# A two-layer encoder trunk on one core: weight splits issued at points from a table, seven products combined in banks by ScalarE copies, first products behind products of the identity

## The chip, the core and the metric

The kernel runs on one of the eight cores of a Trainium2 chip. A core has TensorE (PE, matrix products), VectorE (DVE), ScalarE (ACT), GpSimd (POOL) and SyncE (SP), each with its own queue of instructions, worked off in order. TensorE writes into PSUM, eight banks of 128 partitions x 512 f32; everything else lies in SBUF. Loads and stores are DMAs, issued here mostly by SP, a few by ACT, and those that add to what they find ("accumulating") by POOL.

The metric is the device time of one execution in microseconds, less is better. Before the change it is 919.12 us, the median of three runs (917.77 to 919.91).

## What is computed

256 tokens of width 1024 pass two layers in f32. A layer is half an FFN step, an attention step with two kinds of heads, and another half FFN step; a last normalization follows.

```python
for l in range(DEPTH):                                   # 2
    x = x + 0.5 * swiglu(rms_norm(x, g1), w_gate, w_up, w_down)      # D_FF = 2816
    h = rms_norm(x, mix_norm[l]); proj = h @ w_in[l]                 # q, k, v of both kinds of heads
    x = x + concat([windowed_gqa_sink(...), differential_attention(...)]) @ w_out[l]
    x = x + 0.5 * swiglu(rms_norm(x, g2), w_gate, w_up, w_down)
return rms_norm(x, final_norm)
def swiglu(h, w_gate, w_up, w_down):
    return (silu(h @ w_gate) * (h @ w_up)) @ w_down
```

So there are four FFNs, and they hold most of the products.

## The kernel before

**Split products.** To keep f32 accuracy at the faster format, every operand is split into a high part (ACT casts it, `emit_split`, line 211) and a low part (DVE subtracts the cast from the original, line 212), and a product is made of three matmuls: high x high, low x high, high x low (`tokens`, lines 537 to 539; `prod`, lines 632 to 634). Each weight is loaded once, in blocks of 1 MB (4 chunks of 128 rows x 512 columns); a block is one `Step`, split in two halves ("parts"), each one ACT instruction and one DVE instruction over 128 x 1024.

**Order of the weights.** `specs` is the list of all steps in the order of use. `weights()` (line 249) hands out the next one and calls `ahead(n)` (line 228), which issues, in order of the list, the splits up to part n, the preparations and the DMAs (at most 10 steps ahead and 6 raw blocks at once). How far splits run ahead is one number, `look[0]`: 8 in an FFN, 6 in the attention, with corrections at single places (`less`). `Split.part` (line 182) calls `ahead` once more at the second half of a block.

**Seven products.** FF = 2816 columns are worked in five groups of 512 and a rest of 256. In the groups that `SEVEN` names (2, 3, 4 in the first FFN, 1 to 4 in the other three; 15 in all) the four quarter products of (two blocks of 128 tokens) x (two halves of the inner dimension) for gate and up together are made with seven products of combinations in place of eight. The combinations of x are made once an FFN (`make_sums`, line 349); those of the weights are the blocks a, a+b, b+c, a+b+c and so on, made by accumulating DMAs on POOL (`gather`, line 126) and by DVE adds over 128 x 1024, two a block (`plus`, line 131). `by_seven` (line 637) makes the products in banks of their own, copies two of them to SBUF with ACT (`m1`, `m7`) and combines them with five DVE instructions (`put`, lines 679 to 686) and two that multiply with the silu (`up`, line 616). A group is seven products of 12 matmuls, two down-products of 24 matmuls of the group before (`down`, line 708), and eight transposes of the hidden values (`turn`, line 694), which ACT and DVE split again.

**Banks.** `bank()` (line 71) gives one of eight banks. The four of the down-product (`accs`, line 706) are held through an FFN.

**The start.** ACT's queue issues the four DMAs of x (line 425), 256 KB each, while SP loads the first two weight blocks in chunks of 256 KB (`emit_dma`, lines 155 to 157). `take_x` (line 441) then turns x: for chunks 0 and 1, four transposes each on TensorE, then the operands by ACT (scaled by the gain, line 333) and DVE (line 335); the first products (line 722) come after both. The first Silu comes much later, and with it its table.

**Scheduling.** TensorE's order is always the program's (`Kept`, line 40); that of the other engines too, but for the attention (`kept[0] = False`, line 901), where a scheduler orders them.

Of the kernel before, what the change touches and what calls it, by code (L numbers as in the profile page):

```python
# [9 lines left out]
F32 = mybir.dt.float32  # L10
F32R = mybir.dt.float32r
AF = mybir.ActivationFunctionType
# [18 lines left out]
SEVEN = ((2, 3, 4), (1, 2, 3, 4))  # L31


@with_exitstack
def trunk(ctx: ExitStack, tc: tile.TileContext, x, n1, g1, u1, d1, nm, w_in, sink,
# [35 lines left out]
    def bank():  # L71
        return ps.tile([P, 512], F32, tag="ps", bufs=8, name=nm_("ps"))
# [19 lines left out]
    class Step:  # L92
        def __init__(self, kn, n, moves, key=None, prep=None, src=None, free=None, behind=None):
            self.kn, self.n, self.moves, self.prep = kn, n, moves, prep
            self.behind = behind
            self.key = object() if key is None else key
            self.src = self.key if src is None else src
            self.free = [self.src] if free is None else free
# [16 lines left out]
    def seven(wg, wu, c0, downs, first):  # L115
# [22 lines left out]
        bc = Step(4, 512, load(b), key=b, behind=gather(c, b))  # L138
        rest = [Step(4, 512, load(d), key=d, free=[]), Step(4, 512, load(c), key=c, free=[]), downs[0]]
        steps = [rest[0], rest[2], rest[1], bc] if first else [bc] + rest  # L140
# [3 lines left out]
                Step(4, 512, None, prep=plus(c, a), src=a, free=[c]),  # L144
                Step(4, 512, None, prep=plus(d, a), src=a, free=[a, d]),
                downs[1]]
# [29 lines left out]
    class Split:  # L176


        def __init__(self, i):
            self.i, self.n, self.parts, self.held = i, specs[i].n, [], False  # L180

        def part(self, k, c=slice(None), h=None):

            if h is None:
                h, k = divmod(k, 2)
            if h and not self.held:
                self.held = True
                ahead(2 * self.i + 1 + look[0])
            return [t[:, k, c] for t in self.parts[h]]
# [38 lines left out]
    def ahead(n):  # L228

        n = min(n, 2 * len(specs) - 1)  # L230
        while True:
            if at["split"] <= n and at["prep"] > at["split"] // 2:
# [3 lines left out]
            elif at["prep"] <= min(n // 2 + 1, len(specs) - 1) and at["dma"] > at["prep"] and \  # L236
                    (specs[at["prep"]].prep is None or at["split"] >= 2 * at["prep"]):
# [10 lines left out]

    def weights(less=0, held=False):

        i = at["use"]
        at["use"] += 1
        if i > 1:
            ahead(2 * i + look[0] - less)
        w = loaded[i]
        w.held = held
        return w

    for l in range(DEPTH):
        def ffn_specs(wg, wu, wd, sevens):  # L260
            down = lambda g, h: plain(wd[l], h * 512, 512, 4 * g, 4)
            for k0 in (0, 4):
                specs.extend(plain(w[l], 0, 512, k0, 4) for w in (wg, wu))
            for g in range(1, NGRP):
                downs = [down(g - 1, h) for h in range(2)]
                if g in sevens:
                    specs.extend(seven(wg[l], wu[l], g * 512, downs, g == 1))
                else:
                    specs.extend(plain(w[l], g * 512, 512, k0, 4) for w in (wg, wu) for k0 in (0, 4))
                    specs.extend(downs)  # L270
# [6 lines left out]
            specs.append(down(NGRP - 1, 1))  # L277

# [21 lines left out]
        fine.update(range(mixed + 2, len(specs)))  # L300
        ffn_specs(g2, u2, d2, SEVEN[1])

# [3 lines left out]
    class Norm:  # L306
# [21 lines left out]
        def operands(self, j, sl):  # L328
# [3 lines left out]
            for i, g in enumerate(gs):  # L332
                act.activation(xs[:, i, 0:S], sl[:, i], AF.Identity, scale=g)
            for i, g in enumerate(gs):
                dve.scalar_tensor_tensor(xs[:, i, S:512], in0=sl[:, i], scalar=g, in1=f(xs[:, i, 0:S]),
                                         op0=ALU.mult, op1=ALU.subtract)
            self.turned.append((j, sl, gs))
# [11 lines left out]
        def make_sums(self):  # L349
# [19 lines left out]
            s1 = add(b1, t1, ALU.subtract)  # L369
            s2 = add(s1, t0, ALU.add)  # L370
            yield
            high(s1)
            high(s2)
            yield
            low(0, s1)
            b0_ = add(b0, s2, ALU.subtract)
            low(1, s2)
            v = add(t1, t0, ALU.subtract)
            yield
            high(b0_)  # L380
            high(v)
            yield
            low(2, b0_)
            low(3, v)
# [38 lines left out]
    early = [emit_early(0), emit_early(1)]  # L423
    for j in range(4):
        act.dma_start(xk[:, :, j * 256:(j + 1) * 256], x[0].rearrange("(t p) d -> p t d", p=P)[:, :, j * 256:(j + 1) * 256])
        for e in early:
            next(e)

# [12 lines left out]
    def take_x(k):  # L441

        g, u = early
        if k == 0:
            for j in (0, 1):
                sl = norm.turn(j)
                next(g)
                norm.operands(j, sl)
                next(u)
        elif k == 1:  # L450
            for e in (g, u, g, u):
                next(e)
            norm.squares(0, 0, 512)
            norm.pair(2)
            norm.squares(1, 0, 512)
            ahead(5)
            norm.pair(3)
            norm.squares(0, 512, 512)
        elif k == 2:
            for e in early:  # L460
                next(e, None)
            ahead(7)
            norm.squares(1, 512, 512)
            norm.stats()
            constants()
# [63 lines left out]

    def tokens(accs, xs, w, k0, ks=range(4), first=0, last=KC - 1, order=None, cols=slice(None), h=None):  # L530

        for k, t in (order or [(k, t) for k in ks for t in range(2)]):
            kk = k0 + k
            hi, lo = w.part(k, cols, h)
            xv = xs[kk // 2][:, kk % 2]
            xh, xl = xv[:, t * P:(t + 1) * P], xv[:, S + t * P:S + (t + 1) * P]
# [23 lines left out]
    def first_groups(norm, ws):  # L560

        sls = [halves(bank()) for _ in ws]
# [39 lines left out]
    def ffn(norm, aside=None, before=None, final=False, sevens=SEVEN[1]):  # L602
# [34 lines left out]
        def by_seven(h, g):  # L637


            flat = lambda: tmp().rearrange("p a n -> p (a n)")  # L640

            def put(o, x, y, op):
                dve.tensor_tensor(o, x, y, op=op)
                return o

            late, run = g == max(sevens), 1 in sevens
            m1, m7 = flat(), flat()


            if g > 1:  # L650
                g0 = prod(norm.quarter(0, 0), weights())
                act.copy(m1, g0)
                p7 = prod(norm.summed(3), weights(1, True))
                act.copy(m7, p7)
                hT = turn(h, 2)
                prod(norm.quarter(0, 1), weights(), g0)
                p3 = prod(norm.summed(2), weights())
                if not run:
                    g0 = silu(flat(), g0, 0)
                down(hT, g - 1, 0, weights())  # L660
                if run:
                    g0 = silu(flat(), g0, 0)
            else:
                p1 = prod(norm.quarter(0, 0), weights(1, True))
                hT = turn(h, (0,))
                w = weights(1, True)
                act.copy(m1, p1)
                p2 = prod(norm.quarter(0, 1), w)
                hT += turn(h, (1,))
                g0 = put(flat(), p2, m1, ALU.add)  # L670
                down(hT, 0, 0, weights())
                silu(g0, g0, 0)
                p3 = prod(norm.summed(2), weights())
                p7 = prod(norm.summed(3), weights(1, True))
                act.copy(m7, p7)
# [486 lines left out]
```

## Time and profile before

| | |
|---|---|
| median of three runs | 919.12 us (917.77 to 919.91) |
| the profiled execution | 917.39 us |
| its span, first to last instruction | 915.6 us |
| mean granted TensorE clock | 0.999 |
| HBM read | 199.00 MB, 218 GB/s over the span |

A line of the groups' view reads: line, engine, operation, output tile <- input tiles, shapes, count | busy us, mean ns of one | idle us of the engine just before, and what ended it. In the timeline a line has start, duration and engine, and equal instructions that follow each other are one line with a count. In the chain of waits a line has start, length and what was waited for or ran. In the windows' view each engine has its busy time and, in brackets, its instructions that touch the window. PE is the matmul, PEld the load of its stationary operand, "w" a split weight, "s" a split operand or a hidden value, "raw" a loaded block, "tmp" a combination, "ps" a bank. Nearly every instruction has line 50, that of the helper which records them, so one goes by tiles.

### The profile page before, as it was taken

What the parts mean: (1) busy time and instruction counts of PE and PEld (TensorE: products, weight loads), DVE (VectorE), ACT (ScalarE), POOL (GpSimd) and SP (SyncE); (2) the same over time, 40 slices, a digit from 0 to 9 for tenths busy, and PEclk for the clock granted to TensorE, in tenths of its full rate; (3) what the DMA queues carried; (4) which work ended last, traced back from release to release, by engine and by line L of the source; (5) the groups of instructions that cost most, each with busy time, mean ns of one, the idle gap of its engine ahead of it and who ended that gap; (6) DMA issues with size and microseconds to landing.
All of it is one profiled execution on the core that took longest, in us unless ns stands there. A gap on an engine that the chain in (4) does not pass through costs nothing.

```text
span 915.6 us, 12544 instructions
## 1 busy us (share of the span) xinstructions
PE 904.5 (99%) x4696; PEld 763.7 (83%) x4696; DVE 792.5 (87%) x1096; ACT 589.8 (64%) x917; POOL 66.4 (7%) x83
## 2 busy tenths in 40 slices
PE   8999999999999999999999999999999999999997
PEld 6888888899888888888888888888998888888886
DVE  6768999959975999999789999997797689999994
ACT  7836676557865766576486666665677496666561
POOL 0400100000010100100010010000001010010011
PEclk9999999999999999999999999999999999999999
DMA  9996898828436698898767998887463467998831
GB/s 339 355 238 173 265 297 268 238 93 240 136 108 189 158 280 248 257 273 275 258 164 201 276 285 217 265 293 219 116 230 98 139 153 201 275 289 230 259 132 47
DMA packets 114061, 200.87 MB, mean 219 GB/s; under 512 B 3662, under 2 KB 31376, under 8 KB 114000
## 3 DMA queue, kind: packets, MB, share of 16 engines
q1 hardware_dynamic: 96528, 166.74, 54.5%
q0 software_dynamic: 16096, 31.75, 19.3%
q10 hardware_dynamic: 1376, 1.57, 0.5%
q8 instruction: 37, 0.61, 0.3%
q14 instruction: 24, 0.20, 0.1%
HBM read 199.00 MB, written 1.05 MB: 218 GB/s over the span
## 4 chain that ended last, share of the span: by engine, by line
PE 98%; issue 1%; DMA 0%; ACT 0%; DVE 0%; POOLq 0%; POOL 0%; ACTq 0%
PE ps L50 98%; DMA xk<-in_x_dram 0%; ACT w L50 0%; DVE s L50 0%; DVE xk L50 0%; ACT tmp L50 0%; ACT L50 0%; POOLq L1157 0%; POOL rf L50 0%; ACTq L50 0%; DVE tot L50 0%; DVE tmp L50 0%
## 5 line engine op out<-in xcount | busy, mean ns | idle before, releaser
L50 PE MATMUL ps<-w,s 128*128 128x512 f32 (+1 forms) x2574 | 600.2, 391 | 0.5 <-ACT tmp L50 0.5
L50 PEld LDWEIGHTS ps<-w,s 128*128 128x128 f32 x2574 | 477.6, 188 | 100.3 <-ACT tmp L50 2.3
L50 DVE TENSOR_TENSOR w<-raw,w 128x1024 fp32r<-128x1024 f32 (+1 forms) x458 | 482.1, 1101 | 37.8 <-ACT w L50 36.6
L50 ACT CAST w<-raw 128x1024 fp32r<-128x1024 f32 (+1 forms) x458 | 409.8, 954 | 122.6 <-DVE raw L50 78.4
L50 PE MATMUL ps<-w,q 128*128 128x512 f32 x540 | 127.3, 389 | 0.0
L50 PEld LDWEIGHTS ps<-w,q 128*128 128x128 f32 x540 | 101.4, 188 | 21.0
L50 PE MATMUL ps<-s,w 128*128 128x256 f32 x672 | 83.1, 284 | 0.0
L50 PEld LDWEIGHTS ps<-s,w 128*128 128x128 f32 x672 | 81.5, 192 | 0.5
L50 POOL DMA_DIRECT2D raw<-in_ffn_w_up_dram x30 | 38.9, 1296 | 472.8 <-DVE w L50 240.8
L50 DVE TENSOR_TENSOR raw<-raw,raw 128x1024 f32<-128x1024 f32 x60 | 70.7, 1219 | 0.0
L50 ACT ACTIVATE s<-ps,gcol 128x256 fp32r<-128x256 f32 (+1 forms) x80 | 31.7, 480 | 43.7 <-PE ps L50 42.1
L50 ACT CAST s<-ps 128x512 fp32r<-128x512 f32 x44 | 24.3, 594 | 29.9 <-PE ps L50 29.9
L50 PE MATMUL ps<-w,v 128*128 128x512 f32 x180 | 43.3, 389 | 0.0
L50 ACT COPY tmp<-ps 128x512 f32<-128x512 f32 x34 | 19.9, 585 | 36.2 <-PE ps L50 34.0
L50 ACT ACTIVATE s<-s,negm 128x256 f32<-128x256 f32 x64 | 31.9, 500 | 14.8 <-DVE negm L50 14.8
L50 PE MATMUL ps<-ident,s 128*128 128x128 f32 x304 | 39.7, 273 | 0.0
L50 PEld LDWEIGHTS ps<-w,v 128*128 128x128 f32 x180 | 33.8, 188 | 7.0
L50 PEld LDWEIGHTS ps<-ident,s 128*128 128x128 f32 x304 | 35.1, 140 | 5.1 <-issue 0.8
L50 DVE TENSOR_TENSOR s<-ps,s 128x512 fp32r<-128x512 f32 x44 | 28.7, 686 | 9.1 <-ACT s L50 9.1
L50 DVE SCALAR_TENSOR_TENSOR s<-ps,gcol,s 128x256 fp32r<-128x256 f32 x48 | 20.3, 478 | 11.6 <-ACT s L50 11.5
L50 DVE TENSOR_TENSOR tmp<-ps,tmp 128x512 f32<-128x512 f32 x37 | 25.4, 686 | 2.7 <-PE ps L50 2.1
L50 DVE TENSOR_TENSOR xk<-xk,ps 128x512 f32<-128x512 f32 (+1 forms) x25 | 14.1, 598 | 14.9 <-PE ps L50 14.9
(106 smaller groups left out, 404.7 us busy)
## 6 DMA issues: line engine op xcount, KB each, us to landing
raw<-in_ffn_w_down_dram SPq DMA_DIRECT2D x44, 1024.0 KB, 8.9
raw<-in_ffn_w_gate_dram SPq DMA_DIRECT2D x39, 1024.0 KB, 6.4
raw<-in_ffn_w_up_dram SPq DMA_DIRECT2D x39, 1024.0 KB, 5.7
raw<-in_ffn_w_up_dram POOLq DMA_DIRECT2D x30, 1024.0 KB, 12.3
raw<-in_w_in_dram SPq DMA_DIRECT2D x14, 1024.0 KB, 6.1
raw<-in_ffn_w_gate_dram SPq DMA_DIRECT2D x8, 512.0 KB, 6.2
raw<-in_ffn_w_up_dram SPq DMA_DIRECT2D x8, 512.0 KB, 7.2
raw<-in_w_in_dram SPq DMA_DIRECT2D x8, 512.0 KB, 5.3
```

The source lines that it names most:

```text
L50: ins = issue(*a, **k)
```

## The change

1. **Table of leads.** `LEAD` replaces the one number at named places: a step has `lead = (name, n)`, and `lead()` calls `ahead(2 * i + LEAD[name][2 * n + half])`; inside the seven products `go()` calls it eleven times a group with the next value. `ahead` also holds a split back while an accumulating DMA is still pending.
2. **Seven products in banks.** Six banks stay single (`bank()`), two become one pair (`pair()`). The first product p1 is copied by one ScalarE instruction, negated and broadcast, into both banks of the pair; two later products add there. p1 takes its second product in its own bank, then is overwritten by a ScalarE copy of p5 from bank to bank, and the last product adds to that. DVE makes three combinations in place of five. `plus` is one add over 128 x 2048, block c is loaded later, the transposes go by token (`turn_one`), and the down-product of the second half moves into the next group (`below`), so that it stands between the transposes of the first and the second token block. The signs of the combined x (`make_sums`) change with it. In the FFNs whose first such group is group 1, that group has no earlier one to take a down-product from, and its order is p1, eight transposes, the second product into p1. The pair is also used for other two-bank places in FFN and attention.
3. **The start.** x's first chunk stays on ACT's queue, the other three go to SP, behind four, eight and eight of the weight chunks. A one-element Silu on ACT loads the table. Four products identity x identity go ahead of the transpose of the gains, one after it, two after the transposes of x's chunk 0; then the products of chunk 0 follow (`first_chunk`, in the order high, weight's low, x's low), and only then chunk 1 is turned. The later chunks are turned between products too.

```diff
+LEAD = dict(start=(2, 8, 11, 9),
...
+            mid=(6, 9, 9, 12, 15, 15, 17, 20, 20, 23, 24),
...
     def bank():
-        return ps.tile([P, 512], F32, tag="ps", bufs=8, name=nm_("ps"))
+        return ps.tile([P, 512], F32, tag="ps", bufs=6, name=nm_("ps"))
+
+    def pair():
+        return ps.tile([P, 2, 512], F32, tag="xy", bufs=1, name=nm_("xy"))
...
             def prep():
-                for h in (0, 2):
-                    x_, t_ = [raws[i][:, h:h + 2] for i in (x, to)]
-                    dve.tensor_tensor(t_, t_, x_, op=ALU.add)
+                dve.tensor_tensor(raws[to], raws[to], raws[x], op=ALU.add)
...
+    fetch_x(act, 0)
+    tables = const.tile([P, 1], F32, name="tables")
+    act.activation(tables, ident[:, 0:1], AF.Silu)
     for j in range(4):
-        act.dma_start(xk[:, :, j * 256:(j + 1) * 256], x[0].rearrange("(t p) d -> p t d", p=P)[:, :, j * 256:(j + 1) * 256])
         for e in early:
             next(e)
+        if j == 1:
+            fetch_x(sp, 1)
+    for j in (2, 3):
+        fetch_x(sp, j)
...
+    def keep_busy(n):
+        for _ in range(n):
+            pe.matmul(warm[:, 0:P], lhsT=ident, rhs=ident, start=True, stop=True)
...
+    keep_busy(4)
     pe.transpose(gsl[:, 0:16], grow1, ident[:16, :16])
+    keep_busy(1)
...
+                go()
+                p1 = prod(norm.quarter(0, 0), take())
+                act.activation(xy, p1.unsqueeze(1).to_broadcast([P, 2, 512]), AF.Copy, scale=-1.0)
+                new = [turn_one(h, 0)]
+                go()
+                if start:
+                    new.append(turn_one(h, 1))
+                    go()
+                    prod(norm.quarter(0, 1), take(), p1)
+                else:
+                    below(old, g - 2, 1, take())
+                    new.append(turn_one(h, 1))
+                    go()
+                prod(norm.summed(0), take(), xy[:, 0])
+                go()
+                below(by_token(new), g - 1, 0, take())
+                go()
+                if not start:
+                    prod(norm.quarter(0, 1), take(), p1)
+                g0 = silu(flat(), p1, 0)
+                go()
+                old = by_token(new)
+                p5 = prod(norm.summed(1), take())
+                act.copy(p1, p5)
+                go()
+                prod(norm.summed(2), take(), xy[:, 1])
+                go()
+                prod(norm.summed(3), take(), p5)
+                e = flat()
+                act.copy(e, p5)
+                u1, u0 = flat(), flat()
+                dve.tensor_tensor(u0, xy[:, 1], e, op=ALU.add)
+                dve.tensor_tensor(u1, xy[:, 0], e, op=ALU.add)
+                h = blk(F32)
+                up(h, u0, g0, 0)
+                go()
+                p4 = prod(norm.quarter(1, 1), take(), p1)
+                g1 = flat()
+                dve.tensor_tensor(g1, p4, u1, op=ALU.subtract)
+                go()
+                silu(g1, g1, 1)
+                up(h, u1, g1, 1)
+                go()
```

More of the change, by code (lines that the diff above doesn't have):

```diff
@@ L113, in plain, with seven @@
         return Step(kn, n, lambda t: [(t, src)], **how)
-    def seven(wg, wu, c0, downs, first):
+    def seven(wg, wu, c0, below, down):
         a, b, c, d = [object() for _ in range(4)]
@@ L247, in ahead, with lead @@
                 break
+    def lead(i, half, less=0):
+        s = specs[i]
+        if s.lead is not None:
+            ahead(2 * i + LEAD[s.lead[0]][2 * s.lead[1] + half])
+        else:
+            ahead(2 * i + half + look[0] - less)
     def weights(less=0, held=False):
@@ L253, in weights @@
         if i > 1:
-            ahead(2 * i + look[0] - less)
+            lead(i, 0, less)
+            ahead(2 * i + 1)
         w = loaded[i]
@@ L560, in first_groups @@
     def first_groups(norm, ws):
-        sls = [halves(bank()) for _ in ws]
+        both = pair()
+        sls = [halves(both[:, i]) for i in range(2)]
         for k in range(0, KC, 2):
@@ L937, in mix @@
         vB = tp.tile([P, 2, 512], F32, tag="v", bufs=1, name=nm_("v"))
-        vsl = [bank() for _ in range(2)]
+        both = pair()
+        vsl = [both[:, t] for t in range(2)]
         for k0 in (0, 4):
@@ L984, in mix @@
         oT = [blk() for _ in range(4)]
-        rsl, osl = [[bank() for _ in range(2)] for _ in range(2)]
+        rsl, both = [bank() for _ in range(2)], pair()
+        osl = [both[:, t] for t in range(2)]
         for t in range(2):
```

262 lines of the change are left out of this document (157 added, 105 removed).

## The prediction

> **What bounds the kernel now.** I read the page's first section first (who is busy), then the chain of waits (what the end is made of), then the timeline of the start, because only there does the chain leave TensorE.
>
> ```profile
> span 915.6 us, 12544 instructions
> ...
> PE 904.5 (99%) x4696; PEld 763.7 (83%) x4696; DVE 792.5 (87%) x1096; ACT 589.8 (64%) x917; POOL 66.4 (7%) x83
> ```
>
> ```profile
> 5.70 22.17 PE ps L50 x96
> ...
> 29.00 0.65 ACT L50
> ...
> 30.30 0.70 ACT tmp L50
> ...
> 31.04 873.94 PE ps L50 x4547
> ```
>
> TensorE is busy 99% of the span, and from 31.04 us the chain is one piece of TensorE, 873.94 us long. So an engine made faster elsewhere buys nothing by itself; only fewer TensorE instructions, a faster pace, or shorter pauses count. The instruction orders of the two programs hold the same 3258 products of 512 columns, 902 of 256 columns and the same transposes; the changed one has seven identity products more. TensorE's work does not shrink, so I look for pauses.
>
> ```profile
> 1.01 0.29 POOL masks.py:199 TENSOR_SCALAR_AFFINE_SELECT ident<-ident 128x128 f32<-128x128 f32 x1
> ...
> 3.13 0.26 PE L50 MATMUL ps<-ident,grow 16*128 16x16 f32 x1 [3.13 <-DMA grow<-in_ffn_norm_dram]
> ...
> 3.74 1.12 PE L50 MATMUL ps<-ident,xk 128*128 128x128 f32 x4 [0.35 <-DMA xk<-in_x_dram]
> ...
> 4.99 0.62 ACT L50 CAST w<-raw 128x512 fp32r<-128x512 f32 x1 [0.91 <-DMA raw<-in_ffn_w_gate_dram]
> 5.51 0.83 ACT L50 ACTIVATE s<-ps,gcol 128x256 fp32r<-128x256 f32 x2
> ...
> 5.70 1.11 PE L50 MATMUL ps<-ident,xk 128*128 128x128 f32 x4 [0.85 <-DMA xk<-in_x_dram]
> ...
> 6.47 5.74 PE L50 MATMUL ps<-w,s 128*128 128x512 f32 x19
> ```
>
> ```profile
> 13.18 1.03 PE L50 MATMUL ps<-ident,xk 128*128 128x128 f32 x8
> ...
> 13.97 16.61 PE L50 MATMUL ps<-w,s 128*128 128x512 f32 x72
> ...
> 29.00 1.28 ACT L50 ACT_TABLE_LOAD   x1
> ...
> 31.04 5.30 PE L50 MATMUL ps<-w,s 128*128 128x512 f32 x22 [0.46 <-ACT tmp L50]
> ```
>
> ```profile
> core 0: us, PE busy (x) PEld busy (x) DVE busy (x) ACT busy (x) POOL busy (x), PEclk, DMA share, GB/s
> 6.47:9.08 2.61, 2.61 (x8) 2.01 (x7) 1.88 (x4) 1.63 (x4) 0.00 (x0) 1.00 1.06 399
> 9.08:11.69 2.61, 2.61 (x13) 2.16 (x12) 2.56 (x6) 2.50 (x5) 0.00 (x0) 1.00 1.06 389
> 344.70:375.50 30.80, 30.80 (x141) 25.61 (x140) 30.48 (x32) 19.96 (x24) 2.57 (x2) 1.00 0.92 266
> ```
>
> The first product starts at 6.47 us. Eight matmuls fall in the 2.61 us up to 9.08 and thirteen in the next 2.61 us, so TensorE starts at about half pace, although the clock column says 1.00 in both. The third row is one seven-product group in the steady state: TensorE has no pause, VectorE is busy 30.48 of 30.80 us and still does not hold it up.
>
> **The change part by part.** The pace of one product comes from these rows, and with it the price of the new waits:
>
> ```profile
> 340.87 2.88 PE L50 MATMUL ps<-w,v 128*128 128x512 f32 x12
> ...
> 343.59 1.03 PE L50 MATMUL ps<-ident,s 128*128 128x128 f32 x8
> 343.79 0.59 ACT L50 COPY tmp<-ps 128x512 f32<-128x512 f32 x1 [2.13 <-PE ps L50]
> ...
> 344.38 0.94 PE L50 MATMUL ps<-w,s 128*128 128x512 f32 x3
> ```
>
> Twelve products take 343.59 - 340.87 = 2.72 us, 0.227 each; eight transposes 344.38 - 343.59 = 0.79 us; ScalarE reads a finished bank 0.20 us after the last slot ends.
>
> *The start.* The common point is "24 first products and eight transposes of x done". Before, that is 13.18 us: 6.47 plus 24 x 0.227 = 5.45, plus 1.26 lost to the half pace. After, the order is: five identity products around the transpose of the gains, four transposes of x, two identity products, then the products of chunk 0, and only then the other four transposes. Identity is ready at 1.30. An identity product in f32 is not in the trace; the nearest is
>
> ```profile
> L50 PE MATMUL ps<-v,s 128*128 128x128 f32 x64 | 7.5, 275 | 0.0
> ```
>
> whose 64 records stand for 32 instructions, so two passes each, 7.5/32 = 0.23 us at full pace and perhaps 0.45 at half: four end by 3.15, which is when the gains' DMA lands anyway (3.13); one more, the gains and four transposes at half pace (1.12) end by 5.0, two more by 5.8. All seven cost about 3 us of TensorE, beside the wait for the DMA and for ScalarE, which sets the first product. That one needs the first weight chunk (landed 4.99, a cast of 0.62) and one ScalarE operand (0.83/2 = 0.42). Chunks of 256 KB land 0.7 us apart (4.99, then x's second at 5.70), and x's second to fourth chunk leave ScalarE's queue for SP's, behind four and eight weight chunks; so the first weight chunk comes between 4.3 and 4.99. I take 4.5, so 5.54, and 5.7 with the identity products in front (bounds 5.4 and 6.1). From there 5.45 + 0.44 (four transposes at full pace, 0.11 each) + what half pace is left. TensorE found full pace at about 9.1, 3.4 us after steady work began at 5.70; with work from 1.35 that comes between 4.8 and 8.2, at most (8.2 - 5.7)/2 = 1.25 lost, and I take 0.4. So 12.0 against 13.18: **1.2 us gained** (bounds 0 and 1.9). x's last chunks on SP are not late: all twelve chunks are 3.1 MB, some 8 us at the 389 GB/s of the row above, so there by 12; the transposes that need them stand at 14 and later.
>
> The Trainium skill, "TensorE: Matmul & The Clock Gate", section "What's actually happening", has the array at half clock until one window of about 3.4 us was busy, and the window runs free of the kernel's start. This trace agrees with the 3.4 us; by that rule the identity products save 0 to 1.26 us from run to run, and the sum would be 0.4 better or 0.85 worse, which lies inside the bounds above.
>
> *The Silu table.* Before, 72 products from 13.97 would end at 13.97 + 16.34 = 30.31; TensorE goes on at 31.04, after the table load at 29.00 and the two silus, whose bank it wants. After, a dummy Silu loads the table while ScalarE waits for the first DMA, one load fewer in all, and the silus stand ahead of the casts that waited for a later weight. **0.7 us gained** (0 to 0.73).
>
> *Seven products.* Before, VectorE makes five combinations a group, after, three; ScalarE's copies rise from two of 512 to one of 1024 and two of 512.
>
> ```profile
> 369.57 0.69 DVE L50 TENSOR_TENSOR tmp<-tmp,ps 128x512 f32<-128x512 f32 x1
> 370.29 1.42 DVE L50 SCALAR_TENSOR_TENSOR s<-tmp,hr,tmp 128x512 f32<-128x512 f32 x2
> 371.62 4.63 DVE L50 TENSOR_TENSOR w<-raw,w 128x1024 fp32r<-128x1024 f32 x4
> 376.16 0.69 DVE L50 TENSOR_TENSOR s<-ps,s 128x512 fp32r<-128x512 f32 x1
> ```
>
> By starts, a split costs (376.16 - 371.62)/4 = 1.135, a combination 0.7, a final multiply 0.67. A group has 9 weight blocks: 18 splits 20.4, four half sums (or two whole ones) 4.5, two multiplies 1.35, two subtractions 1.3, and 5 x 0.7 = 3.5 before, 31.1 in all against TensorE's 30.8; after, 3 x 0.7 = 2.1, 29.7. Thirty combinations, 21 us of VectorE, go, and nearly nothing of it is on the path. What is:
>
> ```profile
> PEld ps L50 <- ACT tmp L50: 2.3, 5, 0.9
> ...
> PEld ps L50 <- DVE w L50: 1.2, 4, 0.4
> ```
>
> The four waits for a split, 1.2 us in all, are where VectorE's debt comes due. I take **0.6 us gained** (0 to 1.2), as a weight load's wait is in part hidden by the matmul before it.
>
> *The new wait.* In the first group of the second, third and fourth FFN the copy of -p1 into both banks of the pair must end before the second product adds to p1, and only eight transposes lie between. The copy starts 0.20 after p1, lasts as long as the nearest row of that size,
>
> ```profile
> L50 ACT CAST w<-raw 128x1024 fp32r<-128x1024 f32 x354 | 352.3, 1053 | 120.5 <-DVE raw L50 78.4 <-DMA raw<-in_ffn_w_up_dram 40.3
> ```
>
> 1.05, and 0.05 later TensorE may go (30.30 + 0.70 to 31.04): 1.30 - 0.79 = 0.5 us, three times: **1.5 us lost** (0 if the copy takes half, 4 if ScalarE comes a cast late each time). Behind it on TensorE stands everything; behind the copy on ScalarE the copies of the transposes, needed 5 us later. In all other groups 24 products lie between, 5.4 us, and the wait is covered.
>
> *The whole sums.* One sum of 2048 in place of two of 1024: the cast can't start after the first half, so VectorE idles one cast, 1.0 us, after the second sum of a group: 29.7 + 1.0 = 30.7 against 30.8. It still fits; cost taken as 0, bounds under the rival below. The pair of banks takes two of the eight, used where before two plain banks were; the order of TensorE in the attention is unchanged; the leads from tables shift splits by a few places and I take 0 (-0.3 to +1).
>
> **Sum:** -1.2 - 0.7 - 0.6 + 1.5 = -1.0 us. The profiled execution took 917.39 us (its span of 915.6 and 1.8 around it), so 916.4; that execution is 1.73 under the median of the three runs, 919.12, on which the forecast is put: **918.1 us**.
>
> **The rivals.** *The new wait is covered and the clock is early* (the copy between banks quicker than a cast, first weight chunk at 4.3): -1.5 - 0.4 - 0.3 on the forecast, and up to 0.6 more from the splits: 915.3 to 915.9. Against it: no row has a copy into a bank of that size. *VectorE's order becomes the bound:* slower. Two groups on, the next group's first transposes want the bank of p1, freed when VectorE has made the last combination; by my count that is ready 3.6 us after the sixth product's end and wanted 5.4 us after it, but five splits stand ahead of it in VectorE's order, behind the whole sum; that leaves about 1.1 us. It decides once a group runs over 30.8 us on VectorE: at 0.7 over, the second handover of a run pays 0.3, the third 0.7; at 1.0 over, 0.9 and 1.0. With three runs of four and one of three that is 3.3 to 6.6 us: 921.4 to 924.7. For it: 30.7 of 30.8. Against it: before stood at 31.1 and paid 1.2. *An added DMA holds the cast ahead of the copies:*
>
> ```profile
> raw<-in_ffn_w_up_dram POOLq DMA_DIRECT2D x30, 1024.0 KB, 12.3
> ```
>
> it takes 12.3 us, and ScalarE already waited 40.3 us for those blocks without TensorE's minding; now silu and the copies stand behind, room about 2 us; 0.3 us in eleven groups gives 921.4. *Nothing of it shows:* the start gains 0 as the chunks land as before, the rest cancels: 919.
>
> **How the numbers follow.** Forecast 0.50 (own range 917.0 to 919.2), covered wait 0.22, VectorE's order 0.18, DMA 0.05, nothing 0.05. About 0.2% (1.84 us) is what a measurement of this kernel can tell from no change, so faster means under 917.3. Of the forecast's half, 0.16 lies under that and the rest within; so faster 0.38, same 0.39 and slower 0.23. The range goes from 915.6 to 922.5 and leaves out the dearer half of VectorE's case and little below.
>
> **What would show it.** Right: the first product near 5.7 at full pace soon after, no table load near 29, VectorE about 20 us less busy, and after the first group's eight transposes a TensorE wait of 0.5 us for ScalarE, three times. Wrong: waits for VectorE at the transposes that follow a group, growing along a run; casts waiting for an added DMA with TensorE idle behind; splits late in the attention.

## The result: 916.61 us, and the profile after

| | before | after |
|---|---|---|
| median of 20 runs side by side | 917.89 us (916.69 to 921.05) | 916.61 us (916.06 to 918.08) |
| profiled execution | 917.39 us | 916.47 us |
| its span | 915.6 us | 914.7 us |

The ratio is 0.9982 (95% interval 0.9975 to 0.9988): the change saves 1.65 us of 917.89, 1.1 to 2.3 by the interval; the two medians alone lie 1.28 us apart. The forecast was 1.0 us saved, 918.1 us. Most of the 1.5 us between 918.1 and 916.61 lies in the base: the three runs shown had a median of 919.12, the twenty 917.89. For the profiled execution the forecast was 916.4, and 916.47 came.

The page's first section after the change (the helper line is now 62):

```profile
span 914.7 us, 12449 instructions
...
PE 906.1 (99%) x4710; PEld 766.4 (84%) x4710; DVE 767.5 (84%) x1033; ACT 600.1 (66%) x932; POOL 66.9 (7%) x83
```

TensorE has fourteen records more (seven identity products of two passes) and is as full as before; VectorE has lost 25 us, ScalarE gained 10. As forecast, neither tells where the time came from. The timeline of the start does:

```profile
4.44 0.62 ACT L62 CAST w<-raw 128x512 fp32r<-128x512 f32 x1 [1.71 <-DMA raw<-in_ffn_w_gate_dram]
...
5.79 2.09 PE L62 MATMUL ps<-w,s 128*128 128x512 f32 x6
...
12.31 1.52 PE L62 MATMUL ps<-w,s 128*128 128x512 f32 x6
...
27.28 1.27 ACT L62 ACTIVATE tmp<-ps,r 128x512 f32<-128x512 f32 x2 [0.47 <-POOL r L62]
...
29.56 1.75 PE L62 MATMUL ps<-w,s 128*128 128x512 f32 x7
```

The first product starts at 5.79 (before 6.47). Twenty-four products and eight transposes are done at 12.31 (before 13.18): 0.87 us gained. The silus come at 27.28 without a table load, and the products that stood at 31.04 stand at 29.56: 1.48 us in all, so 0.61 more between the two points.

The windows of the start and of one steady group, with the instructions of each engine in brackets:

```profile
core 0: us, PE busy (x) PEld busy (x) DVE busy (x) ACT busy (x) POOL busy (x), PEclk, DMA share, GB/s
5.79:8.40 2.61, 2.61 (x11) 2.14 (x10) 2.36 (x5) 2.06 (x4) 0.00 (x0) 1.00 1.00 346
8.40:11.01 2.61, 2.61 (x15) 2.16 (x14) 0.92 (x2) 1.27 (x4) 0.00 (x0) 1.00 1.01 352
344.70:375.50 30.80, 30.80 (x141) 25.51 (x140) 29.58 (x28) 21.96 (x26) 2.57 (x2) 1.00 0.91 261
```

From the first product on, eleven matmuls fit in 2.61 us, where before eight did; the half pace ends sooner, and again the clock column does not show it. The trace's own record of the granted clock says why: it begins only where the pace first doubles, at 6.75 us here and at 8.89 before, and the column counts what lies ahead of the record as 1.00. In the steady group VectorE is busy 29.58 of 30.80 us (before 30.48), and TensorE has no pause.

What was paid back stands in the view of waits and, for the first of three places, in the timeline:

```profile
PEld ps L62 <- ACT xy L62: 1.4, 3, 0.5
...
ACT w L62 <- DMA raw<-in_ffn_w_up_dram: 11.2, 2, 10.9
```

```profile
308.28 1.03 PE L62 MATMUL ps<-ident,s 128*128 128x128 f32 x8
308.48 1.01 ACT L62 ACTIVATE xy<-ps 128x1024 f32<-128x1024 f32 x1 [3.35 <-PE ps L62]
309.40 1.08 ACT L62 CAST s<-ps 128x512 fp32r<-128x512 f32 x2
...
309.54 2.79 PE L62 MATMUL ps<-w,s 128*128 128x512 f32 x11 [0.23 <-ACT xy L62]
```

The copy of -p1 lasts 1.01 us; the product behind the eight transposes starts at 309.54, 1.26 after the first of them in place of 0.79: 0.47 us, three times, 1.4 in all. The four waits of weight loads for a split (1.2 us) are gone from the view, and so is most of ScalarE's waiting for the blocks of w_up (40.3 to 11.2 us).

### The profile page after: what moved, and what is told of

Same layout as the page of the kernel before. It is cut to its first block, busy times and chain, and to the rows that moved or that the text cites. A ratio compares the mean times of both kernels' runs of the same rounds, so it can differ in the third digit from the quotient of the medians.

```text
span 914.7 us, 12449 instructions
## 1 busy us (share of the span) xinstructions
PE 906.1 (99%) x4710; PEld 766.4 (84%) x4710; DVE 767.5 (84%) x1033; ACT 600.1 (66%) x932; POOL 66.9 (7%) x83
## 3 DMA queue, kind: packets, MB, share of 16 engines
HBM read 199.00 MB, written 1.05 MB: 219 GB/s over the span
## 4 chain that ended last, share of the span: by engine, by line
PE 98%; issue 0%; ACT 0%; DVE 0%; POOL 0%; POOLq 0%
PE ps L62 73%; PE xy L62 26%; ACT xy L62 0%; DVE s L62 0%; DVE xk L62 0%; POOLq L1291 0%; POOL rf L62 0%; POOL ident masks.py:199 0%; POOL ident masks.py:197 0%; DVE tot L62 0%; POOLq masks.py:199 0%; DVE tmp L62 0%; POOLq L1282 0%
## 5 line engine op out<-in xcount | busy, mean ns | idle before, releaser
L62 PE MATMUL ps<-w,s 128*128 128x512 f32 (+1 forms) x2046 | 478.1, 390 | 0.7 <-ACT xy L62 0.7
L62 PEld LDWEIGHTS ps<-w,s 128*128 128x128 f32 x2046 | 379.4, 188 | 78.9 <-ACT xy L62 1.4
L62 PE MATMUL xy<-w,s 128*128 128x512 f32 x528 | 125.8, 392 | 0.0
L62 PEld LDWEIGHTS xy<-w,s 128*128 128x128 f32 x528 | 98.3, 188 | 20.4
L62 PE MATMUL xy<-w,q 128*128 128x512 f32 x360 | 87.8, 393 | 0.0
L62 PEld LDWEIGHTS xy<-w,q 128*128 128x128 f32 x360 | 66.7, 188 | 13.4
L62 DVE TENSOR_TENSOR raw<-raw,raw 128x2048 f32<-128x2048 f32 x30 | 68.6, 2288 | 0.5
L62 PE MATMUL ps<-s,w 128*128 128x256 f32 x480 | 59.2, 284 | 0.0
L62 PE MATMUL ps<-w,q 128*128 128x512 f32 x180 | 43.2, 389 | 0.0
L62 PEld LDWEIGHTS ps<-w,q 128*128 128x128 f32 x180 | 33.8, 188 | 7.0
```

Source lines behind the costliest of these rows:

```text
L62: ins = issue(*a, **k)
```

## The experiments

All start from the changed kernel. Where a time is set against "the changed kernel", that is 916.61 us (20 runs) or 916.53 (12 more runs, below). The twelve runs were made in three sets of four, each on a chip of its own (first the two engines, the copy twice, no identity products and no early table; last two more instructions, half sums, flat leads and the old order), and the changed kernel was repeated in the second set alone. The kernel before had medians of 918.62, 918.66 and 918.21 us beside them, 917.89 in the result above, so a few tenths of a microsecond between sets prove nothing. The profiles say more: set product by product, behind the start, TensorE's starts in two profiles of these versions keep one distance, within 0.02 us over hundreds of products, and it steps where a wait differs.

**Two engines for the copy.**

```diff
-  act.activation(xy, p1.unsqueeze(1).to_broadcast([P, 2, 512]), AF.Copy, scale=-1.0)
+  if start:
+      act.activation(xy[:, 0], p1, AF.Copy, scale=-1.0)
+      dve.tensor_scalar_mul(xy[:, 1], p1, -1.0)
```

> Theory (the changed kernel pays the new wait in full, 0.5 us at each of three places; with ScalarE copying -p1 into one bank of the pair and VectorE into the other side by side, 0.6 to 0.7 us each in place of 1.01, the copies end with the eight transposes): the three TensorE waits for the copy fall from 0.46 to under 0.1 us, the time falls by 1.0 to 1.5 us on the changed kernel's 916.6, to 915.1 to 915.6. Rival (two engines that read one bank at once slow each other, or VectorE comes late to its copy, so the wait only changes its name): a wait of 0.4 to 0.7 us for VectorE at the same three places, 916.4 to 917.2.

Measured: 917.45 us (916.96 to 917.97), 0.8 more than the changed kernel. The timeline of the first place:

```profile
307.83 1.03 PE L62 MATMUL ps<-ident,s 128*128 128x128 f32 x8
308.03 0.58 ACT L62 ACTIVATE xy<-ps 128x512 f32<-128x512 f32 x1 [3.35 <-PE ps L62]
...
308.64 0.70 DVE L62 TENSOR_SCALAR xy<-ps 128x512 f32<-128x512 f32 x1 [0.66 <-ACT xy L62]
...
309.40 1.89 PE L62 MATMUL ps<-w,s 128*128 128x512 f32 x7 [0.53 <-DVE xy L62]
```

The copies do not run side by side: VectorE waits 0.66 us for ScalarE's and starts when that is over, so 0.58 + 0.70 stand in place of 1.01, and TensorE starts 1.57 after the first transpose in place of 1.26. Three times 0.31 is 0.9: product by product TensorE falls back by 0.31 at each of the three places and nowhere else behind the start, and 0.8 is the time measured. The Trainium skill, "PSUM — Partial Sum Buffer", section "PSUM bank collisions raise a hardware error", says that two engines must not use the same 32-partition quadrant of one bank at once, a read beside a read included, and that the compiler's scheduler puts a dependency between them; the order seen here agrees. This run does not tell whether the shared bank alone made the dependency, since both copies also write the one tile of the pair. So the wait's length counts in full, but this run did not take it away.

**The copy twice.**

```diff
+  for _ in range(2 if start else 1):
       act.activation(xy, p1.unsqueeze(1).to_broadcast([P, 2, 512]), AF.Copy, scale=-1.0)
```

> The copy of -p1 is made twice in a row, in the first group of a run alone. Theory (the wait lies on the path with its whole length): 3 x 1.0 = 3.0 us more, 919.6, and the three waits grow from 0.5 to 1.5 us. Rival (a pause of TensorE there is given back later, since VectorE is the one that really paces a group and catches up in the pause): under 1.5 us more, below 918.1, with TensorE pauses elsewhere in the run gone.

Measured: 919.30 us (919.00 to 920.08), 2.7 to 2.8 more. In the view of waits the same row as before:

```profile
PEld ps L62 <- ACT xy L62: 4.5, 3, 1.5
```

1.4 us became 4.5, and 2.7 of these 3.1 us are found in the time. Product by product TensorE falls back by 1.04 at each of the three places, 3.1 in all, and keeps that to the end: the wait lies on the path with its whole length and is not given back later.

**The second copy later.**

```diff
+  if start:
+      act.activation(xy[:, 0], p1, AF.Copy, scale=-1.0)
...
       new.append(turn_one(h, 1))
+      act.copy(xy[:, 1], xy[:, 0])
```

> In the first group of a run ScalarE copies -p1 into the first bank of the pair alone (0.58 us in the run with two engines, in place of 1.01) and copies that bank to the second one after the two casts of the transposes; TensorE wants the second bank much later. Theory (the three waits stand wholly on the path and depend on how long p1 is read): TensorE waits 0.0 to 0.1 us in place of 0.46 at the three places, 1.0 to 1.4 us less than the changed kernel beside it. Rival (the later copy holds the weight casts behind it back by 0.6 us and a split comes late): the three pauses move to the next products, within 0.3 us of the changed kernel.

Measured: **915.29 us** (914.97 to 915.75), 1.24 under the changed kernel beside it; against the kernel before, 0.9967 (0.9955 to 0.9979). The timeline:

```profile
308.60 1.03 PE L62 MATMUL ps<-ident,s 128*128 128x128 f32 x8
308.80 0.58 ACT L62 ACTIVATE xy<-ps 128x512 f32<-128x512 f32 x1 [3.34 <-PE ps L62]
...
309.43 3.01 PE L62 MATMUL ps<-w,s 128*128 128x512 f32 x12
...
310.24 0.62 ACT L62 COPY xy<-xy 128x512 f32<-128x512 f32 x1
```

The product starts 0.83 after the first transpose, 0.43 sooner; three times, 1.3 us, and that is what TensorE's starts gain between the two profiles. p1 is read for half as long, and the second bank is filled from the first while twelve products run. This is the fastest of the versions.

**No identity products.**

```diff
-  keep_busy(4)
   pe.transpose(gsl[:, 0:16], grow1, ident[:16, :16])
-  keep_busy(1)
...
-  keep_busy(2)
```

> The seven identity products are left out. Theory (they bring TensorE to full pace early): first product between 5.4 and 5.8, but half pace until about 8 to 9 us in place of 6.8, so 24 products and eight transposes done 0.5 to 1.0 us later than 12.31; 917.1 to 917.6. Rival (the pace at the start follows its own clock or comes with the first long products, and the start gained by its order and its transfers alone): done within 0.3 us of 12.31, or earlier by the 0.2 to 0.5 us that the products take; 916.1 to 916.8.

Measured: 918.01 us (916.87 to 918.60), 1.4 to 1.5 more. The first product stands where it did, and the windows from there show the pace:

```profile
5.80:8.41 2.61, 2.59 (x6) 2.11 (x7) 2.59 (x6) 1.98 (x4) 0.00 (x0) 1.00 1.02 351
8.41:11.02 2.61, 2.61 (x9) 2.00 (x9) 0.44 (x1) 0.00 (x0) 0.00 (x0) 1.00 1.03 363
```

```profile
5.82 2.93 PE L62 MATMUL ps<-w,s 128*128 128x512 f32 x6 [0.62 <-ACT s L62]
...
14.03 1.52 PE L62 MATMUL ps<-w,s 128*128 128x512 f32 x6
```

Six and nine matmuls in place of eleven and fifteen; the common point of 24 products is at 14.03 in place of 12.31. The seven idle products do not bring the first product forward; they bring the full pace forward. By the trace's clock record it came at 10.52 us here, at 8.89 in the kernel before, which has none of them either, and between 4.93 and 8.08 in the twelve profiles that have them. The size is less sure: 1.7 us between these two executions, 1.4 to 1.5 between medians of different sets.

**The changed kernel again**, unaltered.

> The changed kernel, unaltered, beside the others of this call, to compare with them on one chip. Theory (the pace of the first products changes at a moment that differs from execution to execution, as the four profiles so far show, 12 to 5 half-paced products and fewer): 0.1 to 0.3% under the kernel before, with the time itself spread over 1 to 2 us. Rival (the gain belonged to the first chip): within 0.1% of the kernel before.

Measured: 916.53 us (915.72 to 918.14), ratio 0.9978 (0.9970 to 0.9987). Its first product came at 6.01: with nothing changed the first loads landed later, the first weight chunk at 4.94 in place of 4.42, so that landing moves by 0.5 us by itself. The change of pace moves by more. In the twelve profiles with the identity products the clock record begins between 4.93 and 8.08 us (in five of them ahead of the first weight product, so that none is at half pace), and the common point lies between 11.83 and 12.91.

**x on ScalarE's queue.**

```diff
-  fetch_x(sp, 1)
+  fetch_x(act, 1)
...
-  fetch_x(sp, j)
+  fetch_x(act, j)
```

> All four chunks of x go out on ScalarE's queue again, as before the change; the rest is as changed. Theory (the first product waits for the first weight chunk, and that landed earlier since x's other chunks left for SP's queue): the first weight chunk lands at 4.8 to 5.0 in place of 4.42, the first product at 6.1 to 6.4 in place of 5.79, 0.3 to 0.6 us lost. Rival (the order of the work alone, products of chunk 0 ahead of the transposes of chunk 1, brought the start): first product at 5.8 to 5.9, nothing lost.

Measured: 916.79 us (916.08 to 917.24), 0.26 over the kernel beside it, inside the spread.

```profile
4.51 0.62 ACT L62 CAST w<-raw 128x512 fp32r<-128x512 f32 x1 [1.78 <-DMA raw<-in_ffn_w_gate_dram]
...
5.70 1.66 PE L62 MATMUL ps<-w,s 128*128 128x512 f32 x6
```

The cast of the first weight chunk starts at 4.51 in place of 4.44, and the first product at 5.70. Over all profiles of the changed kernel and its versions that cast starts between 4.44 and 4.99 with x's other chunks on SP's queue, and at 4.51 and 4.73 in the two with them on ScalarE's. The queue of x's chunks brought nothing that shows.

**The old order of the start**, with x on ScalarE's queue as above, and chunk 1 turned and made an operand ahead of the first product:

```diff
   norm.operands(0, sl, lambda: next(u))
+  norm.pair(1)
   next(g)
```

> x on ScalarE's queue as before and both its first chunks turned and made operands ahead of the first product, as before; the identity products and the rest as changed. Theory (the order, not the queue, brought the first product forward): first product at 6.2 to 6.6 in place of 5.7 to 6.0, and 24 products with eight transposes done 0.3 to 0.8 us later than in the changed kernel at an equal pace; 916.8 to 917.4. Rival (the transposes only change places with the products, and fill the wait for the first chunk): first product up to 0.5 us later, the common point equal within 0.2 us; 916.3 to 916.8.

Measured: 916.96 us (916.00 to 917.50), 0.35 to 0.43 more.

```profile
5.49 0.60 PE L62 MATMUL ps<-ident,xk 128*128 128x128 f32 x4
5.85 1.63 PE L62 MATMUL ps<-w,s 128*128 128x512 f32 x6
...
9.66 1.21 PE L62 MATMUL ps<-w,s 128*128 128x512 f32 x4 [0.26 <-DVE w L62]
```

The transposes of chunk 1 fit before the first product, which comes at 5.85. What is lost is later: the operands of chunk 1 stand ahead of a weight's split, and TensorE waits for it at 9.66. At full pace from the first product on, the common point is 12.10 against 11.84 in the run just above: the order is worth 0.26 us or less, since here the first chunk's cast also starts 0.22 later. My theory had the place wrong (the first product), the size nearly right.

**No early table.**

```diff
-  act.activation(tables, ident[:, 0:1], AF.Silu)
```

> The one-element Silu is left out, so the table is loaded by the first real Silu near 27 us. Theory (the load was what kept TensorE waiting before the second group): TensorE pauses 0.5 to 0.9 us at about 29.6 for ScalarE; 917.1 to 917.5. Rival (the silus now stand ahead of the casts and have 1.3 us to spare, so the load is covered): no pause at 29.6 over 0.1 us; 916.3 to 916.8.

Measured: 916.64 us (916.23 to 917.40), no difference from 916.61. The timeline does show one:

```profile
26.79 1.28 ACT L62 ACT_TABLE_LOAD   x1
28.09 1.26 ACT L62 ACTIVATE tmp<-ps,r 128x512 f32<-128x512 f32 x2
...
33.73 1.40 DVE L62 SCALAR_TENSOR_TENSOR s<-xy,hr,tmp 128x512 f32<-128x512 f32 x2
...
35.19 0.98 PE L62 MATMUL ps<-ident,s 128*128 128x128 f32 x7 [0.27 <-DVE s L62]
```

The load is back, the silus come 0.8 us later, and TensorE pauses, not at 29.6 but at the hidden values' transposes at 34.6 and 35.2: there its starts fall back by 0.61 us against the changed kernel's, and stay so. That execution had no half-paced product, which hides 0.5 of it; why the median of twelve runs shows nothing stays open. The 0.6 us is shown by one execution, not by the times; by these alone the rival, a load that is covered, would stand.

**Four more VectorE instructions a group.**

```diff
   up(h, u1, g1, 1)
+  for _ in range(4):
+      dve.tensor_tensor(e, e, u0, op=ALU.add)
```

> Four idle additions over 128 x 512 at the end of each of the fifteen groups, on VectorE, some 0.6 us each, 2.4 us a group: 29.5 + 2.4 = 31.9 of 30.8. Theory (what VectorE was relieved of is worth only what a group runs over TensorE's 30.8 us): over by 1.1 us a group from the second group of a run on, less the reserve built up before, so 4 to 12 us more than the changed kernel, with TensorE waiting for VectorE's splits or for the banks after a handover. Rival (VectorE has far more reserve, since splits run several places ahead): under 1 us more.

Measured: 947.18 us (945.78 to 948.20), 30.6 more; far beyond the 4 to 12 expected. The groups' view and the waits:

```profile
L62 DVE TENSOR_TENSOR tmp<-tmp,tmp 128x512 f32<-128x512 f32 x60 | 41.4, 690 | 1.5
```

```profile
PE ps L62 <- DVE s L62: 21.1, 16, 2.3
```

41.4 us of idle work cost 30.6. One addition lasts 0.69, not 0.6, and a group's reserve is smaller than the 1.2 us that busy times show: by the starts of its instructions TensorE loses 1.6 us at the first handover, from group to group, of a run and 2.4 at each later one (a later one in the timeline below), for 2.8 us of additions, so the reserve comes out as 1.2 us at first and then 0.4 a group.

```profile
380.96 0.65 PE L62 MATMUL ps<-ident,s 128*128 128x128 f32 x4 [2.27 <-DVE s L62]
```

**Two more.** The same with `range(2)`: as many instructions as the change took from each group, though at the group's end and not where the removed ones stood.

> Two idle additions over 128 x 512 a group, which is what the change took from VectorE (0.7 us each by starts). Theory, mended after the run with four (2.8 us a group gave TensorE pauses of 1.6 us at the first handover of a run and 2.4 at the later ones, so the reserve is 1.2 us at first and 0.4 a group then): 1.4 us a group give 0.2 and then 1.0 us, some 7 to 9 us in all on the changed kernel's 916.5, 923 to 926. Rival (the relief is worth what the old kernel paid in waits for splits): 0.6 to 1.2 us, 917.1 to 917.7.

Measured: 925.63 us (924.93 to 925.97), 9.1 more, at the upper end of the mended theory. TensorE's starts lose 0.5 to 0.6 us at the first handover of each of the three runs of four groups, where the theory had 0.2, and 0.9 to 1.0 at each later one. One later handover, first in the changed kernel, then here:

```profile
365.04 0.60 PE L62 MATMUL ps<-ident,s 128*128 128x128 f32 x4
...
369.32 0.68 DVE L62 TENSOR_TENSOR s<-ps,s 128x512 fp32r<-128x512 f32 x1
...
370.95 0.60 PE L62 MATMUL ps<-ident,s 128*128 128x128 f32 x4
```

```profile
371.67 0.69 DVE L62 TENSOR_TENSOR tmp<-tmp,tmp 128x512 f32<-128x512 f32 x1
372.28 1.22 DVE L62 TENSOR_TENSOR w<-raw,w 128x1024 fp32r<-128x1024 f32 x1
373.42 0.68 DVE L62 TENSOR_TENSOR s<-ps,s 128x512 fp32r<-128x512 f32 x1
...
374.16 0.66 PE L62 MATMUL ps<-ident,s 128*128 128x128 f32 x4 [0.76 <-DVE s L62]
```

The transposes of the second token block start when VectorE has read the bank of the first block's transposes (the split "s<-ps"): in the changed kernel 0.95 us after that split ends, here at once, after 0.76 us of waiting. By the code the four banks of the down-products leave two of the six single ones, one of which holds p1; so the second block's transposes take the first one's bank.

**Half sums**, as before the change (`plus` over 2 x 1024).

> The sums of weights over 2 x 1024 in place of 2048, as before the change. Theory (a whole sum costs VectorE one idle cast a group, which the reserve of 0.4 us covers): no TensorE pause comes or goes in the groups, within 0.3 us of the changed kernel's 916.5. Rival (the halves, with one more fixed cost each, 0.1 us, and another order of cast and sum, eat the reserve): pauses for VectorE at handovers, 0.5 to 3 us more.

Measured: 916.08 us (915.60 to 916.97), 0.45 to 0.5 under the changed kernel, ratio 0.9979 (0.9971 to 0.9988), no more than the sets differ by. No TensorE pause came or went in the groups: its starts lie 0.16 us ahead of the changed kernel's in the first FFN and 0.18 at the end. VectorE's window is the same:

```profile
344.70:375.50 30.80, 30.80 (x141) 25.54 (x140) 29.55 (x30) 22.07 (x26) 2.57 (x2) 1.00 0.90 261
```

**Flat leads.**

```diff
 def lead(i, half, less=0):
-    if s.lead is not None:
+    if False:
```

This puts the old numbers, 8 and 6, at the new places; it isn't the old rule, since calls at the second half of held blocks stay.

> The leads of the table at the opening and the end of an FFN and in the attention are replaced by the one number of before; those inside the seven products stay. Theory (the waits for splits went because VectorE has less to do): within 0.3 us of 916.5, no new TensorE wait for a split. Rival (they went because the table issues those splits sooner): waits for splits of 0.5 to 1.5 us in all come back near the opening and the end of the FFNs, 917.0 to 918.0.

Measured: 942.03 us (941.30 to 943.18), 25.5 more; both theories fall. The start's timeline:

```profile
15.74 2.19 ACT L62 CAST w<-raw 128x512 fp32r<-128x512 f32 x4 [2.63 <-DMA raw<-in_ffn_w_gate_dram]
...
23.88 1.99 ACT L62 CAST w<-raw 128x1024 fp32r<-128x1024 f32 x2 [0.72 <-DMA raw<-in_ffn_w_gate_dram]
...
25.77 0.83 ACT L62 ACTIVATE s<-ps,gcol 128x256 fp32r<-128x256 f32 x2
26.29 0.80 PE L62 MATMUL ps<-w,s 128*128 128x512 f32 x1 [7.63 <-ACT s L62]
```

It is not splits that come late but splits that come too early in ScalarE's order: casts of blocks that have not landed stand ahead of the operands of x's third chunk, and TensorE waits 7.6 us. The products behind that pause run at half pace again, eight in 3 us, and here the clock column shows it (0.50, after the count of POOL):

```profile
29.00:32.00 3.00, 3.00 (x8) 2.32 (x8) 1.72 (x5) 2.19 (x4) 2.14 (x4) 0.50 1.07 391
```

At the first groups of the later FFNs TensorE's starts fall back by 2.9 to 3.3 us for hidden values, and half pace follows each time:

```profile
319.89 1.05 ACT L62 CAST w<-raw 128x1024 fp32r<-128x1024 f32 x1 [1.99 <-DMA raw<-in_ffn_w_up_dram]
320.97 1.23 DVE L62 TENSOR_TENSOR w<-raw,w 128x1024 fp32r<-128x1024 f32 x1 [3.12 <-ACT w L62]
322.12 1.41 DVE L62 SCALAR_TENSOR_TENSOR s<-xy,hr,tmp 128x512 f32<-128x512 f32 x2
...
323.01 1.94 PE L62 MATMUL ps<-ident,s 128*128 128x128 f32 x8 [2.76 <-DVE s L62]
```

VectorE's two multiplications stand behind a split, the split behind a cast, and the cast waits for its block to land.

## Why the prediction was right, and where its steps were not

- **What bounds the kernel: right.** Only pauses, and the pace at the start, counted. But "nearly nothing of it is on the path", of VectorE's 21 us, holds for the old order alone. In the changed order two such instructions a group cost 9.1 us when they are put back: the new order needs the relief in order not to lose. What the relief gained against the old kernel is not shown by itself. The four split waits went, but with two instructions put back they stay away and TensorE pauses at the handovers, so the leads or the new order may have removed them.
- **The start, 1.2 us forecast, 0.87 measured; the reason was partly wrong.** The step "x's second to fourth chunk leave ScalarE's queue for SP's [...] so the first weight chunk comes between 4.3 and 4.99" failed as a cause: the cast of that chunk starts at 4.51 with x on ScalarE's queue, and the chunk lands at 4.94 in a repetition of the changed kernel, so the landing's 0.5 us was taken from one execution. The half pace, put at 0.4 us lost, is the larger part: the identity products are worth 1.4 to 1.5 us in the median, the order 0.26 or less. The bounds for full pace, 4.8 to 8.2 us, held the whole spread that was seen, 4.93 to 8.08, though "about 9.1" in the kernel before was the edge of a window of the view: by the clock record it is 8.89, 3.2 us after 5.70. That this execution lost 0.5 us to the half pace (12.31 against 11.83 in one without), and not 0 or 1.1, is chance. By the Trainium skill's page "TensorE: Matmul & The Clock Gate", section "What's actually happening", the point of change differs from run to run because the window runs free; the spread of 3.15 us over twelve profiles agrees with a window of 3.4, but not with the 0.5 us to either side that the section gives for that point.
- **The Silu table, 0.7 forecast, 0.61 in the profile.** Without the early load a pause of 0.6 us comes back, though at the hidden values' transposes; the median of that run does not show it.
- **Seven products, 0.6 forecast, about 0.7 in the profiles:** the four waits of 1.2 us are gone. They stood at the last groups of the third and fourth FFN, at 598.7, 600.3, 872.3 and 873.8 us, and set product by product TensorE's starts gain some 0.17 us at each. Two waits for a ScalarE copy beside them (at 567.3 and 871.6), which the sum did not have, went too, for another 0.4. Whether fewer instructions, the leads or the order removed these waits stays open, as no run has the old order with the new number of instructions.
- **The new wait, 1.5 forecast, 1.24 measured** by the run without it, 1.3 by TensorE's starts in the two profiles, 1.4 by the stretches above. Its price came from the cast of the nearest size (1.05 against 1.01 us), and it was fully on the path, as doubling showed.
- **Whole sums, 0: right**, by the run with half sums.
- **Leads, 0 (-0.3 to +1):** no run has the old rule in the new order, so this term was not measured. The table as such is far from worth nothing there: the old numbers cost 25.5 us.
- **The rivals.** "VectorE's order becomes the bound" did not happen, but the kernel stands only 0.4 us a group from it (the count of 30.7 against 30.8 left 0.1). Its prices were good: at 1.0 us over, it gave 0.9 and 1.0 at the later handovers, and with two additions (1.4 less 0.4) TensorE's starts lose 0.92 to 1.02 there; the first handover, which it had free, costs 0.5 to 0.6. Its place was not right: it is the second block's transposes that wait, for the bank of the first block's, not the first transposes for the bank of p1. "The new wait is covered" fell with the trace. "An added DMA holds the cast" fell with the 40.3 us of waiting that became 11.2. "Nothing of it shows" fell with the interval, 0.9975 to 0.9988.

Together, product by product from the two profiles: 0.87 + 0.61 gained up to 29.56 us, 0.14 more right behind; 1.3 lost at three places; 1.1 gained at the last groups of the third and fourth FFN, 0.7 of it at the split waits; 0.3 gained at the beginnings of the two attention steps, at the first of which the old kernel's transposes wait 0.2 us for VectorE; and some 0.5 lost in steps of up to 0.1. The last TensorE instruction starts 1.16 us earlier. That this lies so near the forecast's 1.0 is in part luck: the start came out 0.33 short, and gains that the sum did not have, at ScalarE's copies and in the attention, made up for it.

## What to carry to other kernels

A copy out of a bank that the next product changes costs its whole length less what TensorE has between: make the first reader short, and fill further banks from its copy. Where TensorE is never idle, work taken from another engine may show no gain and still be what the new order lives on; put it back in idle form to learn the reserve, for the busy share (29.6 of 30.8 us) made it three times too large. Where an engine works its queue in order, a prefetch issued too early does harm: a cast that waits for its DMA holds what stands behind it (25.5 us with flat leads).

## What the runs showed of the hardware that was not expected

- TensorE's half pace at the start ended at a moment that differed by 3 us (4.93 to 8.08) between executions of kernels that begin with the same identity products, worth up to 1.1 us at the common point (11.83 to 12.91). The column of the granted clock reads 1.00 there, as its record begins only at that moment, so the pace at the start has to be read from counts of matmuls in a window.
- After a pause of 7.6 us, and after each of the three of 2.8 to 3.1 us, the next products ran at half pace again (with flat leads), which adds to the price of a long wait. The clock record has these stretches as 10.24 us and three of 3.41; 10.24 is three times 3.41. With four more instructions a group, one pause of 2.2 us was followed by such a stretch of 3.41, four others of 2.2 to 2.3 were not.
- Two engines' copies from one bank into two others were made one after the other (0.58, then 0.70 us): VectorE's waited for ScalarE's.
- VectorE's real reserve was 0.4 us a group where its busy time left 1.2: what counts is the one instruction that frees a bank, and what stands ahead of it.
